# First layer of a two-layer hybrid decoder on one core: the norm's column on ScalarE, low parts issued behind the next block, rope angles mostly on ScalarE, x's sums all on VectorE

## Chip, cores and metric

One Trainium2 chip, one core of it. The metric is the device time of one execution in microseconds (us), as the median of three runs. The profiler records one further execution of the same program.

## What is computed

Two layers over 512 tokens (S) with 2048 features (D). The change lies in the first lines of the first layer; the rest is cut.

```
cos, sin = rope_tables(positions, x.dtype)
c_act = jax.nn.silu(c)
for l in range(DEPTH):
    mod = c_act @ ada_w[l] + ada_b[l]
    shift, scale, gate = [m[:, None, :] for m in jnp.split(mod, 3, axis=-1)]
    h = rms_norm(x, norm_g[l]) * (1.0 + scale) + shift
    z = h @ w_in[l]
    ...      # latent attention and a conv module, both gated, from pieces of z
    y = jnp.concatenate([mla_out, conv_out], axis=-1) @ w_out[l]
    x = x + gate * y
```

## The kernel before

**Layout.** Features lie on the 128 partitions and tokens on the free axis, so x and h are 16 blocks of 128x512, called *columns* here (j from 0 to 15). fp32 products are made of three fp32r matmuls: weights and h are each split into a high part (`hi`, a rounded copy) and a low part (`lo`, the rest), and `mm3` (L249 to L251) adds hi·hi, hi·lo and lo·hi.

**The modulation of a column (layer 0).** `scale0(j)` loads 128 rows of `ada_w` (1 MB) for the scale of column j; `Gemv.block` multiplies them with the broadcast silu(c) and sums, one VectorE instruction (`ada`, L336) and a small one that reads the sum. `make_gs` (L350, `mod<-mod,avec`, 128x1) turns the sum into (1 + scale)·norm_g on VectorE. A second block, `g.block(0, j)`, gives the shift. Then `make_h`: x times gain times 1/rms on VectorE (L356, `x`), the high part with the shift on ScalarE (L357, `h`), the low part on VectorE (L358, `h`), which reads the high part. So each column costs VectorE two blocks, `mod`, `x` and the low part.

**The weights of a column.** `chunk` loads 128x1024 weights (0.5 MB, `raw`), casts them to `hi` on ScalarE in two halves (L242), subtracts for `lo` on GpSimd (L243, the queue that is named SENG) and issues 24 matmuls into 8 PSUM tiles. A *chunk* below is this for one column and one set of 8 output tiles. There are 24: three columns of the first set (K1 = 3), whose sums are then copied out to `held`; eight columns of the gate set (KH = 8), copied out to `part`; then columns 3 to 15 of the first set, added to `held` (L458). `modulate_to` puts the columns ahead of the chunks at rates MR0 and MR, so that a column is made for every one to two chunks.

**The head.** `rope_angles` reduces the position angles on VectorE (13 instructions), `rope_tables` takes two sines on ScalarE. `first_x` squares x's 16 columns on ScalarE and adds them up: the first four on GpSimd, the others on VectorE in two sums. `token_rsqrt_bc` turns the sums into 1/rms (TensorE sums, small VectorE instructions `sm`, `dg`, TensorE again).

**What sets the order.** Each engine runs its own list in order; the lists are made by a scheduler from the order of the code and from its own guess of durations, so a line of code can stand earlier or later on its engine than it was written. All loads go through SyncE's queue in order; `ada` has three buffers, `raw` four, `hi` and `lo` five halves each.

Of the kernel before, what the change touches and what calls it, by code (L numbers as in the profile page):

```python
# [9 lines left out]
F32 = mybir.dt.float32  # L10
# [6 lines left out]
P = 128  # L17
# [33 lines left out]
def hybrid_trunk(ctx, tc, xT, c, pos, invf, vec, adaT, w_s, w_t, w_kr, w_q, w_kv, w_pw, w_o, outT):  # L51
# [22 lines left out]
    def r4(n):  # L74
        return big.tile([P, 2, S], F32R, tag="r4", name=nm(n))
# [43 lines left out]
    def ms(n):  # L119
        return f2(n, "m", NM)  # L120
# [25 lines left out]

    def rope_angles():


        iv = cp.tile([P, 1], F32, tag="iv", name="iv")  # L150
        nc.sync.dma_start(out=iv, in_=invf)
        posi = sp.tile([P, S], I32, tag="t", bufs=3, name="posi")
        nc.sync.dma_start(out=posi, in_=pos.partition_broadcast(P))
        ang, rd = sinT, cosT
        V.tensor_copy(out=ang, in_=posi)
        V.tensor_scalar(out=ang, in0=ang, scalar1=iv, scalar2=None, op0=ALU.mult)
        V.tensor_scalar(out=rd, in0=ang, scalar1=1.0 / TWO_PI, scalar2=MAGIC, op0=ALU.mult, op1=ALU.add)
        V.tensor_scalar(out=rd, in0=rd, scalar1=MAGIC, scalar2=None, op0=ALU.subtract)
        for cc in (C1, C2, C3):
            V.scalar_tensor_tensor(out=ang, in0=rd, scalar=-cc, in1=ang, op0=ALU.mult, op1=ALU.add)  # L160
        V.tensor_scalar(out=ang, in0=ang, scalar1=3.1415925, scalar2=-3.1415925, op0=ALU.min, op1=ALU.max)
        V.tensor_scalar(out=rd, in0=ang, scalar1=-1.0, scalar2=None, op0=ALU.mult)
        V.tensor_max(out=rd, in0=rd, in1=ang)
        V.tensor_scalar(out=rd, in0=rd, scalar1=-1.0, scalar2=math.pi / 2, op0=ALU.mult, op1=ALU.add)
        for p0 in (0, 64):
            V.tensor_scalar(out=ang[p0:p0 + 32], in0=ang[p0:p0 + 32], scalar1=-1.0, scalar2=None, op0=ALU.mult)

    def rope_tables():
        A.activation(out=sinT, in_=sinT, func=AF.Sin)
        A.activation(out=cosT, in_=cosT, func=AF.Sin)  # L170


    def rsqrt_small(x, y, t, scaled=True):
# [190 lines left out]
    def square_sum(acc, x, j, eng=None):  # L364
        if j == 0:
            A.activation(out=acc, in_=x, func=AF.Square)
        else:
            sq = f2("sq")[:, 0:x.shape[1]]
            A.activation(out=sq, in_=x, func=AF.Square)
            (eng or V).tensor_tensor(out=acc, in0=acc, in1=sq, op=ALU.add)  # L370


    def first_x():
        xs = []
        accs = [ms("acc") for _ in range(3)]
        for j in range(0, KC, 2):
            t = r4f("x")
            nc.sync.dma_start(out=t, in_=xT[j:j + 2].rearrange("k p t -> p k t"))
            for e in range(2):

                acc = accs[2] if j < 4 else accs[e]
                square_sum(acc, t[:, e], j + e if j < 4 else j - 4, nc.gpsimd if j < 4 else V)
                xs.append(t[:, e])
        V.tensor_add(out=accs[0], in0=accs[0], in1=accs[2])
        V.tensor_add(out=accs[0], in0=accs[0], in1=accs[1])
        return xs, accs[0]

    def layer(l, xs, rstd, rpsum):
        last = l == DEPTH - 1
# [31 lines left out]
        if l == 0:  # L421
            def modulated(j):
                if j >= EARLY:
                    scale0(j)
                g.block(0, j)
                h.append(make_h(0, j, xs[j], rstd if j else rpsum[0]))

            def park(tiles, where):
                for n in range(8):
                    p = where(n)  # L430
                    (A.copy if n % 2 else V.tensor_copy)(out=p, in_=tiles[n])
                    yield p

            def modulate_to(m):
                while len(h) < min(int(m), KC):
                    if len(h) < NI:
                        with tc.issue_after(rstd_ins.ins):
                            modulated(len(h))
                    else:
                        modulated(len(h))  # L440

            first = [psum(t, "z") for t in tags]
            for j in range(K1):
                modulate_to(j + 1)
                chunk(first, w_first(j), h[j], j == 0, j == K1 - 1)
            held = list(park(first, lambda n: ms("held") if n < 2 else f2("held", "held", 6, sp)))
            mg = [psum(t, "z") for t in tags]
            for j in range(KH):
                modulate_to(max(j + 1, K1 + MR0 * (j + 1)))
                chunk(mg, w_t[l, 0:H, :, j, :].rearrange("a p b -> p a b"), h[j], j == 0, j == KH - 1)  # L450
            part = list(park(mg, lambda n: ms("part")))
            first = [psum(t, "z") for t in tags]
            for j in range(K1, KC):
                modulate_to(max(j + 1, K1 + MR0 * KH + MR * (j + 1 - K1)))
                chunk(first, w_first(j), h[j], j == K1, j == KC - 1)
            krw = kr_weights()
            for n in range(8):
                V.tensor_add(out=held[n], in0=first[n], in1=held[n])  # L458
                first[n] = held[n]
        else:  # L460


            ws = []
            for j in range(2):
                raw = load_w(w_first(j), 8, P)
                ws.append([split_w(raw[:, q:q + 4], SENG, extra[0] if j and q else None) for q in (0, 4)])
                h.append(r4("h"))
            first = [psum(t, "z") for t in tags[:7]]

            def early(n, tk):  # L470
                for j in range(2):
                    hi, lo = ws[j][n // 4]
                    mm3(first[n][:, tk], hi[:, n % 4], lo[:, n % 4], h[j][:, 0, tk], h[j][:, 1, tk], j == 0, False)

            for i, (tk, rs) in enumerate(zip(HALF, rpsum)):
                for j in range(2):
                    make_h(l, j, xs[j], rs if j == 0 else rstd[:, tk], h[j], tk)
                for j in range(2):
                    for n in range(7):
                        hi, lo = ws[j][n // 4]  # L480
# [626 lines left out]
```

## Time and profile before

| | before |
|---|---|
| median of three runs | 1667.66 us (1665.26 to 1672.59) |
| profiled execution, its own time | 1668.02 us |
| span in the profile | 1666.2 us |
| granted TensorE clock, mean of the span | 0.987 |
| busy: TensorE matmul, VectorE, ScalarE, GpSimd | 95%, 74%, 41%, 40% |
| first matmul of a chunk starts, last one of the 24 chunks ends | 34.27 us, 193.43 us |

The span runs from the first to the last instruction; 1.8 us of the time lie around it. A busy TensorE is not one at its peak: its matmuls overlap. Shares over the whole span say little of a change that touches only the first 190 us; that stretch has to be read by itself.

### The profile page before, as it was taken

To read this page: it belongs to the slowest core of one execution; us is meant where nothing else is said; L and a number is where in the kernel's file an instruction comes from. 1 tells how busy PE (TensorE), PEld (TensorE's weight loads), DVE (VectorE), ACT (ScalarE), POOL (GpSimd) and SP (SyncE) were. 2 spreads that over 40 slices of the span, in tenths; PEclk is the share of its full clock that TensorE was granted. 3 is DMA by queue.
4 is the path that set the end of the run, shared out by engine and by line. 5 is a ranking of instruction groups with operands and counts; after the bars stand their busy time and mean duration, and the time that the engine had idled before them with its cause. 6 is when DMAs were issued, how large, how long until landed. Compare 5 with 4: busy or idle time off the path is not lost.

```text
span 1666.2 us, 20654 instructions
## 1 busy us (share of the span) xinstructions
PE 1581.1 (95%) x7350; PEld 1300.9 (78%) x7350; DVE 1226.2 (74%) x2008; ACT 687.4 (41%) x1284; POOL 659.7 (40%) x440
## 2 busy tenths in 40 slices
PE   4988999999999989999999899999999998999999
PEld 2766778877888878788887678888787887888888
DVE  8898897889999558766549675777788787784332
ACT  4222455554654335322223264545445443532221
POOL 2565633425233455666625554331434335100000
PEclk9999999999999999999999999999999999999999
DMA  8877323223233644898936613322332355565441
GB/s 304 287 278 286 135 90 100 70 83 86 76 114 98 231 152 167 287 335 296 322 98 228 246 64 108 92 92 80 99 93 70 104 170 211 177 236 198 151 142 62
DMA packets 82890, 271.53 MB, mean 163 GB/s; under 512 B 10721, under 2 KB 21729, under 8 KB 70241
## 3 DMA queue, kind: packets, MB, share of 16 engines
q1 hardware_dynamic: 82786, 270.20, 48.1%
q8 instruction: 58, 0.95, 0.2%
q14 instruction: 46, 0.38, 0.1%
HBM read 257.55 MB, written 12.62 MB: 162 GB/s over the span
## 4 chain that ended last, share of the span: by engine, by line
PE 62%; DVE 28%; ACT 6%; issue 3%; DMA 1%; POOL 1%; SPq 0%; POOLq 0%; ACTq 0%; DVEq 0%
DVE ada L336 7%; PE wo L250 7%; PE wo L251 7%; PE wo L249 7%; DVE cv L547 5%; PE z L249 4%; PE z L251 4%; PE z L250 4%; PE cg L249 3%; PE cg L251 3%; PE cg L250 3%; PE mg L251 2%; PE mg L249 2%; PE mg L250 2%; DVE x L356 2%
## 5 line engine op out<-in xcount | busy, mean ns | idle before, releaser
L243 POOL TENSOR_TENSOR lo<-raw,hi 128x512 fp32r<-128x512 f32 x380 | 595.2, 1581 | 657.5 <-ACT hi L242 647.3
L242 ACT CAST hi<-raw 128x512 fp32r<-128x512 f32 (+1 forms) x512 | 307.1, 611 | 518.0 <-PE wo L250 209.6
L547 DVE SCALAR_TENSOR_TENSOR cv<-u,lvec,cv 128x512 f32<-128x512 f32 x464 | 348.6, 751 | 7.4
L249 PE MATMUL z<-h,hi 128*128 128x512 f32 (+1 forms) x782 | 305.8, 396 | 17.2 <-ACT h L357 11.0
L251 PE MATMUL z<-h,lo 128*128 128x512 f32 (+1 forms) x782 | 305.8, 391 | 8.3 <-POOL lo L243 8.3
L250 PE MATMUL z<-h,hi 128*128 128x512 f32 (+1 forms) x782 | 304.6, 390 | 0.8 <-DVE h L358 0.7
L336 DVE CUSTOM_DVE_ANT_0 ada<-ada,cb,avec 128x2048 f32<-128x2048 f32 x96 | 257.4, 2682 | 40.5 <-DMA ada<-in_adaT_dram 40.4
L249 PE MATMUL wo<-cat,hi 128*128 128x512 f32 (+1 forms) x544 | 205.8, 378 | 2.0 <-ACT cat L944 2.0
L250 PE MATMUL wo<-cat,hi 128*128 128x512 f32 (+1 forms) x544 | 206.3, 379 | 1.1 <-DVE cat L945 1.0
L251 PE MATMUL wo<-cat,lo 128*128 128x512 f32 (+1 forms) x544 | 205.8, 378 | 0.0
L249 PEld LDWEIGHTS z<-h,hi 128*128 128x128 f32 x782 | 148.5, 191 | 49.2 <-ACT h L357 13.4
L251 PEld LDWEIGHTS z<-h,lo 128*128 128x128 f32 x782 | 148.4, 190 | 42.9 <-POOL lo L243 13.3
L250 PEld LDWEIGHTS z<-h,hi 128*128 128x128 f32 x782 | 148.6, 190 | 29.3 <-DVE h L358 1.8
L243 DVE TENSOR_TENSOR lo<-raw,hi 128x512 fp32r<-128x512 f32 (+1 forms) x132 | 86.3, 655 | 95.0 <-ACT hi L242 94.7
L249 PEld LDWEIGHTS wo<-cat,hi 128*128 128x128 f32 x544 | 102.9, 189 | 21.2 <-ACT cat L944 2.4
L250 PEld LDWEIGHTS wo<-cat,hi 128*128 128x128 f32 x544 | 102.9, 189 | 21.2 <-DVE cat L945 2.3
L251 PEld LDWEIGHTS wo<-cat,lo 128*128 128x128 f32 x544 | 103.0, 189 | 18.8
L249 PE MATMUL cg<-h,hi 128*128 128x512 f32 x256 | 103.0, 402 | 0.0
L250 PE MATMUL cg<-h,hi 128*128 128x512 f32 x256 | 101.5, 397 | 0.0
L251 PE MATMUL cg<-h,lo 128*128 128x512 f32 x256 | 101.5, 396 | 0.0
L780 ACT ACTIVATE pr<-pr,smx,sc 128x128 f32<-128x128 f32 (+1 forms) x64 | 41.9, 654 | 122.8 <-DVE smx L779 122.7
L357 ACT ACTIVATE h<-x,mod 128x512 fp32r<-128x512 f32 (+1 forms) x34 | 23.3, 697 | 136.8 <-DVE mod L336 100.5
(265 smaller groups left out, 2543.4 us busy)
## 6 DMA issues: line engine op xcount, KB each, us to landing
ada<-in_adaT_dram SPq DMA_DIRECT2D x96, 1024.0 KB, 5.7
raw<-in_w_t_dram SPq DMA_DIRECT2D x120, 512.0 KB, 3.8
raw<-in_w_o_dram SPq DMA_DIRECT2D x64, 512.0 KB, 4.6
raw<-in_w_s_dram SPq DMA_DIRECT2D x32, 512.0 KB, 5.9
raw<-in_w_pw_dram SPq DMA_DIRECT2D x16, 512.0 KB, 3.6
raw<-in_w_q_dram SPq DMA_DIRECT2D x24, 256.0 KB, 2.7
x<-in_xT_dram SPq DMA_DIRECT2D x8, 512.0 KB, 6.8
kf<-kfd SPq DMA_DIRECT2D x16, 256.0 KB, 3.7
```

What stands on the lines that cost most here:

```text
L242: A.copy(out=hiv, in_=rawv)
L243: i = eng.tensor_tensor(out=lov, in0=rawv, in1=f(hiv), op=ALU.subtract)
L249: T.matmul(out=ps, lhsT=whi, rhs=mhi, start=start, stop=False)
L250: T.matmul(out=ps, lhsT=whi, rhs=mlo, start=False, stop=False)
L251: T.matmul(out=ps, lhsT=wlo, rhs=mhi, start=False, stop=stop)
L336: V.tensor_tensor_reduce(out=t, in0=t, in1=self.cb, scale=1.0, scalar=vv(l, "ada_b", b), op0=ALU.mult, op1=ALU.add, accum_out=mods[l][:, b ...
L356: V.scalar_tensor_tensor(out=x, in0=x, scalar=gs(l, j), in1=rstd, op0=ALU.mult, op1=ALU.mult)
L357: A.activation(out=hi, in_=x, func=AF.Identity, bias=shift(l, j))
L547: V.scalar_tensor_tensor(out=box[-1], in0=u[:, k:k + S], scalar=w, in1=box[0], op0=ALU.mult, op1=ALU.add)
L780: A.activation(out=pr[:, :n], in_=pr[:, :n], func=AF.Exp, scale=scl, bias=nb, accum_out=sums)
```

## The change

Four edits, all in the head and in layer 0. (1) `scale0` makes the gain on ScalarE (an activation with scale and bias, 128x1) in place of `make_gs` on VectorE. (2) The low part of a column is kept back in `pending` and written in the code after the next column's scale block (`begin`, `settle`). (3) `rope_angles` leaves the first product of the angles to ScalarE and drops the last five VectorE instructions; `rope_tables` does abs, two sines and two negations on ScalarE, issued after the first high part. (4) `first_x` adds all squares on VectorE in two sums; the low parts of the weights of chunk 0 are made on VectorE.

```diff
@@ rope_angles, rope_tables
-        V.tensor_copy(out=ang, in_=posi)
-        V.tensor_scalar(out=ang, in0=ang, scalar1=iv, scalar2=None, op0=ALU.mult)
+        A.activation(out=ang, in_=posi, func=AF.Copy, scale=iv)
...
-        V.tensor_scalar(out=rd, in0=ang, scalar1=-1.0, scalar2=None, op0=ALU.mult)
-        V.tensor_max(out=rd, in0=rd, in1=ang)
-        V.tensor_scalar(out=rd, in0=rd, scalar1=-1.0, scalar2=math.pi / 2, op0=ALU.mult, op1=ALU.add)
+    def rope_tables():
+
+        A.activation(out=cosT, in_=sinT, func=AF.Abs)
+        A.activation(out=cosT, in_=cosT, func=AF.Sin, scale=-1.0, bias=half_pi)
+        A.activation(out=sinT, in_=sinT, func=AF.Sin)
         for p0 in (0, 64):
-            V.tensor_scalar(out=ang[p0:p0 + 32], in0=ang[p0:p0 + 32], scalar1=-1.0, scalar2=None, op0=ALU.mult)
...
+            A.activation(out=sinT[p0:p0 + 32], in_=sinT[p0:p0 + 32], func=AF.Copy, scale=-1.0)
@@ first_x
-                acc = accs[2] if j < 4 else accs[e]
-                square_sum(acc, t[:, e], j + e if j < 4 else j - 4, nc.gpsimd if j < 4 else V)
+                square_sum((acc, acc2)[e], t[:, e], j)
@@ layer
-        def chunk(tiles, src, hj, start, stop):
+        def chunk(tiles, src, hj, start, stop, eng=SENG):
...
+            def begin(j):
+                if j < KC and j == begun[0]:
+                    begun[0] += 1
+                    scale0(j)
...
             def modulated(j):
-                if j >= EARLY:
-                    scale0(j)
+
+                begin(j)
+                settle()
                 g.block(0, j)
-                h.append(make_h(0, j, xs[j], rstd if j else rpsum[0]))
+                t, r = r4("h"), rstd if j else rpsum[0]
+                hi, lo, x = t[:, 0], t[:, 1], xs[j]
+                V.scalar_tensor_tensor(out=x, in0=x, scalar=gs(0, j), in1=r, op0=ALU.mult, op1=ALU.mult)
+                hi_ins[0] = A.activation(out=hi, in_=x, func=AF.Identity, bias=shift(0, j))
+                pending.append(lambda: V.scalar_tensor_tensor(out=lo, in0=x, scalar=shift(0, j), in1=f(hi),
+                                                              op0=ALU.add, op1=ALU.subtract))
+                h.append(t)
...
+                if j == len(h) - 1 and pending:
+                    if j:
+                        begin(j + 1)
+                    settle()
...
-                chunk(first, w_first(j), h[j], j == 0, j == K1 - 1)
+                modulate_to(j + 1, j)
+                if j == 0:
+                    with tc.issue_after(hi_ins[0].ins):
+                        rope_tables()
+                chunk(first, w_first(j), h[j], j == 0, j == K1 - 1, SENG if j else V)
@@ scale0
         g.block(0, 16 + j)
-        make_gs(0, j)
+        n = vv(0, "norm_g", j)
+        A.activation(out=gs(0, j), in_=gs(0, j), func=AF.Identity, scale=n, bias=n)
```

The order that this makes on the engines is shown at three places. In the rows, `ada` is a block (ISA, 128x2048) and the short row behind it reads its sum; line numbers above L154 differ between the two kernels.

**VectorE, columns 0 and 1.** Before, from the scale block of column 1 (`ada_285`):

```order
L336 ISA ada_285,mod_122<-ada_285,cb_126,avec_120 128x2048
L336 ISA mod_122 128x1
L358 SCALAR_TENSOR_TENSOR h_247<-x_144,mod_122,h_247 128x512
L350 SCALAR_TENSOR_TENSOR mod_122<-mod_122,avec_120 128x1
L356 SCALAR_TENSOR_TENSOR x_144<-x_144,mod_122,rstd_208 128x512
L336 ISA ada_289,mod_122<-ada_289,cb_126,avec_120 128x2048
L336 ISA mod_122 128x1
L358 SCALAR_TENSOR_TENSOR h_292<-x_144,mod_122,h_292 128x512
```

and now, from the same block (`ada_284`):

```order
L336 ISA ada_284,mod_118<-ada_284,cb_122,avec_116 128x2048
L336 ISA mod_118 128x1
L439 SCALAR_TENSOR_TENSOR h_241<-x_139,mod_118,h_241 128x512
L336 ISA ada_288,mod_118<-ada_288,cb_122,avec_116 128x2048
L336 ISA mod_118 128x1
L437 SCALAR_TENSOR_TENSOR x_139<-x_139,mod_118,rstd_204 128x512
L336 ISA ada_294,mod_118<-ada_294,cb_122,avec_116 128x2048
L336 ISA mod_118 128x1
L439 SCALAR_TENSOR_TENSOR h_291<-x_139,mod_118,h_291 128x512
```

The `mod` of column 1 is gone, and between column 1's shift block (`ada_288`) and its low part (`h_291`) there now stand `x` and the scale block of column 2 (`ada_294`).

**VectorE, columns 4 and 5.** Before, from the scale block of column 4 (`ada_512`) on:

```order
L336 ISA ada_512,mod_122<-ada_512,cb_126,avec_120 128x2048
L336 ISA mod_122 128x1
L350 SCALAR_TENSOR_TENSOR mod_122<-mod_122,avec_120 128x1
L356 SCALAR_TENSOR_TENSOR x_158<-x_158,mod_122,rstd_208 128x512
L336 ISA ada_516,mod_122<-ada_516,cb_126,avec_120 128x2048
L336 ISA mod_122 128x1
L358 SCALAR_TENSOR_TENSOR h_519<-x_158,mod_122,h_519 128x512
L336 ISA ada_557,mod_122<-ada_557,cb_126,avec_120 128x2048
```

and now, from the same block (`ada_510`) on:

```order
L336 ISA ada_510,mod_118<-ada_510,cb_122,avec_116 128x2048
L336 ISA mod_118 128x1
L437 SCALAR_TENSOR_TENSOR x_151<-x_151,mod_118,rstd_204 128x512
L336 ISA ada_515,mod_118<-ada_515,cb_122,avec_116 128x2048
L336 ISA mod_118 128x1
L439 SCALAR_TENSOR_TENSOR h_518<-x_151,mod_118,h_518 128x512
L336 ISA ada_555,mod_118<-ada_555,cb_122,avec_116 128x2048
```

Only `mod` has gone: the low part of column 4 stands directly behind its own shift block and ahead of the scale block of column 5, as before; columns 5 to 15 read alike, but for column 8, where one copy to `part` stands between the two.

**ScalarE, columns 4 and 5** (`h` is the high part of a column, `hi` the cast of half a chunk's weights). Before, from the high part of column 4:

```order
L357 ACTIVATE h_519<-x_158,mod_122 128x512
L242 CAST hi_570<-raw_568 128x512
L242 CAST hi_586<-raw_568 128x512
L357 ACTIVATE h_564<-x_158,mod_122 128x512
L242 CAST hi_604<-raw_602 128x512
L242 CAST hi_620<-raw_602 128x512
```

and now:

```order
L438 ACTIVATE h_518<-x_151,mod_118 128x512
L1061 ACTIVATE mod_118<-mod_118,avec_116 128x1
L242 CAST hi_568<-raw_566 128x512
L242 CAST hi_584<-raw_566 128x512
L438 ACTIVATE h_563<-x_151,mod_118 128x512
L242 CAST hi_607<-raw_605 128x512
L242 CAST hi_623<-raw_605 128x512
```

The casts keep their places between the high parts, but the first pair now stands behind `mod`, which reads the sum of column 5's scale block.

## Rows read from the trace of the kernel before

**Rows 1.** The page: busy us (share of the span) and instructions of each engine.

```profile
PE 1581.1 (95%) x7350; PEld 1300.9 (78%) x7350; DVE 1226.2 (74%) x2008; ACT 687.4 (41%) x1284; POOL 659.7 (40%) x440
```

**Rows 2.** Windows: us, busy per engine (instructions), granted clock, DMA share, GB/s.

```profile
33.00:110.00 77.00, 66.92 (x269) 52.87 (x270) 68.70 (x61) 22.53 (x39) 43.32 (x22) 0.98 0.84 287
110.00:193.50 83.50, 75.88 (x311) 59.46 (x310) 73.51 (x63) 23.65 (x43) 52.06 (x29) 0.96 0.69 250
```

**Rows 3.** Waits of VectorE, 30 to 195 us: total us, times, longest.

```profile
DVE h L358 <- ACT h L357: 11.9, 15, 0.8
```

**Rows 4.** Groups by line, VectorE, 30 to 187 us: busy us, mean ns.

```profile
L336 DVE CUSTOM_DVE_ANT_0 ada<-ada,cb,avec 128x2048 f32<-128x2048 f32 x31 | 87.1, 2809 | 0.0
L350 DVE SCALAR_TENSOR_TENSOR mod<-mod,avec 128x1 f32<-128x1 f32 x15 | 15.0, 997 | 0.4
```

**Rows 5.** Timeline of column 13, VectorE, with GpSimd's pairs: start us, us.

```profile
159.52 1.12 DVE L350 SCALAR_TENSOR_TENSOR mod<-mod,avec 128x1 f32<-128x1 f32 x1
160.68 0.75 DVE L356 SCALAR_TENSOR_TENSOR x<-x,mod,rstd 128x512 f32<-128x512 f32 x1
161.35 2.35 DVE L336 CUSTOM_DVE_ANT_0 ada<-ada,cb,avec 128x2048 f32<-128x2048 f32 x1
164.49 0.75 DVE L358 SCALAR_TENSOR_TENSOR h<-x,mod,h 128x512 fp32r<-128x512 f32 x1 [0.79 <-ACT h L357]
165.16 3.37 DVE L336 CUSTOM_DVE_ANT_0 ada<-ada,cb,avec 128x2048 f32<-128x2048 f32 x1
...
155.99 4.64 POOL L243 TENSOR_TENSOR lo<-raw,hi 128x512 fp32r<-128x512 f32 x2 [3.50 <-ACT hi L242]
165.04 7.57 POOL L243 TENSOR_TENSOR lo<-raw,hi 128x512 fp32r<-128x512 f32 x4 [4.42 <-ACT hi L242]
```

**Rows 6.** Timeline around column 3, VectorE, and one GpSimd instruction.

```profile
58.20 0.15 DVE L350 SCALAR_TENSOR_TENSOR mod<-mod,avec 128x1 f32<-128x1 f32 x1
60.53 1.77 DVE L356 SCALAR_TENSOR_TENSOR x<-x,mod,rstd 128x512 f32<-128x512 f32 x1
63.10 0.91 DVE L358 SCALAR_TENSOR_TENSOR h<-x,mod,h 128x512 fp32r<-128x512 f32 x1 [0.79 <-ACT h L357]
...
61.72 1.75 POOL L243 TENSOR_TENSOR lo<-raw,hi 128x512 fp32r<-128x512 f32 x1
```

**Rows 7.** Timeline of the head, and the page's group of low parts on VectorE.

```profile
22.44 0.69 DVE L385 TENSOR_TENSOR acc<-acc,acc 128x512 f32<-128x512 f32 x1
23.19 1.87 PE L194 MATMUL st<-ones,acc 128*128 128x1 f32 x8 [9.22 <-DVE acc L385]
25.44 1.09 DVE L350 SCALAR_TENSOR_TENSOR mod<-mod,avec 128x1 f32<-128x1 f32 x1
26.53 1.23 DVE L176 TENSOR_SCALAR sm<-sm 128x4 int32<-128x4 int32 x1
32.71 0.75 DVE L356 SCALAR_TENSOR_TENSOR x<-x,mod,stb 128x512 f32<-128x512 f32 x1 [0.57 <-ACT rstd L222]
...
L243 DVE TENSOR_TENSOR lo<-raw,hi 128x512 fp32r<-128x512 f32 (+1 forms) x132 | 86.3, 655 | 95.0 <-ACT hi L242 94.7
```

**Rows 8.** Timeline: scale sums of columns 4 and 15, last matmuls of the chunks.

```profile
67.25 0.07 DVE L336 DVE_READ_ACCUMULATOR2_ANT mod<- 128x1 f32 x1
179.54 0.07 DVE L336 DVE_READ_ACCUMULATOR2_ANT mod<- 128x1 f32 x1
192.81 0.39 PE L250 MATMUL z<-h,hi 128*128 128x512 f32 x1
193.04 0.39 PE L251 MATMUL z<-h,lo 128*128 128x512 f32 x1
```

**Rows 9.** Groups of ScalarE: one element per partition, and 128.

```profile
L780 ACT ACTIVATION_READ_ACCUMULATOR pr<-pr,smx,sc 128x1 f32 x64 | 12.0, 187 | 0.0
L782 ACT ACTIVATE pr<-pr,smx 128x128 f32<-128x128 f32 x16 | 6.4, 400 | 2.0 <-DVE smx L781 2.0
```

**Rows 10.** DMA issues, 33 to 190 us: KB each, median us to landing.

```profile
raw<-in_w_s_dram SPq DMA_DIRECT2D x14, 512.0 KB, 6.2
```

More of the change, by code (lines that the diff above doesn't have):

```diff
@@ L161, in rope_angles @@
         V.tensor_scalar(out=ang, in0=ang, scalar1=3.1415925, scalar2=-3.1415925, op0=ALU.min, op1=ALU.max)
-        V.tensor_scalar(out=rd, in0=ang, scalar1=-1.0, scalar2=None, op0=ALU.mult)
-        V.tensor_max(out=rd, in0=rd, in1=ang)
-        V.tensor_scalar(out=rd, in0=rd, scalar1=-1.0, scalar2=math.pi / 2, op0=ALU.mult, op1=ALU.add)
+    half_pi = cp.tile([P, 1], F32, tag="half_pi", name="half_pi")
+    V.memset(half_pi, math.pi / 2)
+    def rope_tables():
+        A.activation(out=cosT, in_=sinT, func=AF.Abs)
+        A.activation(out=cosT, in_=cosT, func=AF.Sin, scale=-1.0, bias=half_pi)
+        A.activation(out=sinT, in_=sinT, func=AF.Sin)
         for p0 in (0, 64):
-            V.tensor_scalar(out=ang[p0:p0 + 32], in0=ang[p0:p0 + 32], scalar1=-1.0, scalar2=None, op0=ALU.mult)
-    def rope_tables():
-        A.activation(out=sinT, in_=sinT, func=AF.Sin)
-        A.activation(out=cosT, in_=cosT, func=AF.Sin)
+            A.activation(out=sinT[p0:p0 + 32], in_=sinT[p0:p0 + 32], func=AF.Copy, scale=-1.0)
     def rsqrt_small(x, y, t, scaled=True):
@@ L374, in first_x @@
         xs = []
-        accs = [ms("acc") for _ in range(3)]
+        acc, acc2 = ms("acc"), ms("acc2")
         for j in range(0, KC, 2):
@@ L379, in first_x @@
             for e in range(2):
-                acc = accs[2] if j < 4 else accs[e]
-                square_sum(acc, t[:, e], j + e if j < 4 else j - 4, nc.gpsimd if j < 4 else V)
+                square_sum((acc, acc2)[e], t[:, e], j)
                 xs.append(t[:, e])
-        V.tensor_add(out=accs[0], in0=accs[0], in1=accs[2])
-        V.tensor_add(out=accs[0], in0=accs[0], in1=accs[1])
-        return xs, accs[0]
+        V.tensor_add(out=acc, in0=acc, in1=acc2)
+        return xs, acc
     def layer(l, xs, rstd, rpsum):
@@ L395, in layer @@
         tags = [t for t in ("mm", "up", "s", "cv", "pz") for _ in range(NB[t])]
-        def chunk(tiles, src, hj, start, stop):
+        def chunk(tiles, src, hj, start, stop, eng=SENG):
             raw = load_w(src, 8, P)
             for q in (0, 4):
-                hi, lo = split_w(raw[:, q:q + 4], SENG)
+                hi, lo = split_w(raw[:, q:q + 4], eng)
                 for n in range(4):
@@ L421, in layer, with settle @@
         if l == 0:
+            pending, begun = [], [EARLY]
+            def begin(j):
+                if j < KC and j == begun[0]:
+                    begun[0] += 1
+                    scale0(j)
+            def settle():
+                while pending:
+                    pending.pop()()
             def modulated(j):
-                if j >= EARLY:
-                    scale0(j)
+                begin(j)
+                settle()
                 g.block(0, j)
-                h.append(make_h(0, j, xs[j], rstd if j else rpsum[0]))
+                t, r = r4("h"), rstd if j else rpsum[0]
[5 more added lines that the diff above has]
+                h.append(t)
+            hi_ins = [None]
             def park(tiles, where):
@@ L432, in park, with modulate_to @@
                     yield p
-            def modulate_to(m):
+            def modulate_to(m, j):
                 while len(h) < min(int(m), KC):
@@ L440, in modulate_to @@
                         modulated(len(h))
+                if j == len(h) - 1 and pending:
+                    if j:
+                        begin(j + 1)
+                    settle()
             first = [psum(t, "z") for t in tags]
             for j in range(K1):
-                modulate_to(j + 1)
-                chunk(first, w_first(j), h[j], j == 0, j == K1 - 1)
+                modulate_to(j + 1, j)
[3 more added lines that the diff above has]
+                chunk(first, w_first(j), h[j], j == 0, j == K1 - 1, SENG if j else V)
             held = list(park(first, lambda n: ms("held") if n < 2 else f2("held", "held", 6, sp)))
@@ L448, in layer @@
             for j in range(KH):
-                modulate_to(max(j + 1, K1 + MR0 * (j + 1)))
+                modulate_to(max(j + 1, K1 + MR0 * (j + 1)), j)
                 chunk(mg, w_t[l, 0:H, :, j, :].rearrange("a p b -> p a b"), h[j], j == 0, j == KH - 1)
@@ L453, in layer @@
             for j in range(K1, KC):
-                modulate_to(max(j + 1, K1 + MR0 * KH + MR * (j + 1 - K1)))
+                modulate_to(max(j + 1, K1 + MR0 * KH + MR * (j + 1 - K1)), j)
                 chunk(first, w_first(j), h[j], j == K1, j == KC - 1)
@@ L1041, in hybrid_trunk @@
     state = (xs, rstd0, [token_rsqrt_bc(acc, D, rstd0)])
-    rope_tables()
     rstd_ins = bc_ins[0]
```

## Prediction

> **What bounds the kernel now.** The page comes first: TensorE is 95% busy over the span, VectorE 74% [rows 1]. For this change the average is of no use, since all that is edited lies ahead of 193.43 us [rows 8]. So I cut that stretch into windows. From 33 to 110 us VectorE is busy 68.70 of 77.00 us, from 110 to 193.5 us 73.51 of 83.50 [rows 2]: some 89%. TensorE shows 66.92 and 75.88, but its matmuls overlap. The starts of its last two lie 0.23 us apart [rows 8], so the 24 chunks of 24 matmuls need 576 x 0.23 = 132 us of the 159 us from the first of them at 34.27 us to the last at 193.43 us. VectorE sets the pace; TensorE has some 27 us of idle time and of slower matmuls.
>
> What does VectorE lose? Two things. The list of its waits shows 11.9 us in 15 waits of 0.79 us: the low part waits until ScalarE has made the high part of the same column [rows 3]. And by the groups, a block takes 2.81 us in the mean, the 128x1 `mod` 1.00 us [rows 4]. The timeline tells why: a block takes 2.35 or 3.37 us [rows 5], `mod` 0.15 us while GpSimd is idle and 1.12 us behind a GpSimd pair [rows 5, 6]. Each is longer by about 1.0 us when a GpSimd subtraction is pending. In column 13 the pair that began at 155.99 ends with the slow `mod`; the next `x` takes its plain 0.75 [rows 5]. With GpSimd idle, `mod` took 0.15, and the `x` two instructions on paid, with 1.77 us [rows 6]. So the price belongs to the GpSimd instruction, not to the VectorE instruction that it meets. One case costs little: the subtraction from 61.72 to 63.47 us ran mostly under the 0.79 us wait, and the low part took 0.91 us, 0.16 more than 0.75 [rows 5, 6].
>
> The Trainium skill has this as a rule (SBUF, "Who interferes with whom"): a VectorE instruction with two SBUF inputs and a GpSimd instruction that reads SBUF take the shared pair of ports one after the other, for a whole instruction each. It speaks against this change, since a 128x1 `mod` that leaves VectorE does not take the GpSimd instruction with it. The trace agrees on who pays, with 0.97 to 1.02 us per stall. In the sum below the rule would alter nothing, as both sides hold the same number of stalls.
>
> **The change part by part.**
>
> *Head.* VectorE has its last sum at 23.13 us now [rows 7]. With two sines off the middle of ScalarE's squares and one closing addition of 0.69 us less, and with four more additions on VectorE, which has that time once seven angle instructions (some 5.5 us) are gone, I put it about 1.0 us earlier. The chain behind it then loses the `mod` of 1.09 us, and some 1.0 us of the 1.23 us of `sm`, one more stall beside GpSimd [rows 7], since the low parts of chunk 0 no longer run there; so -2.1 us. But the first block, which overlapped TensorE's 1.87 us of sums, now stands behind them, +1.9, and the two low parts on VectorE, 0.655 us each [rows 7], stand ahead of `x`, +1.3, of which the 0.57 us wait there covers a part. Sum: -1.0 - 2.1 + 1.9 + 1.3 - 0.6 = -0.5, and I take **-0.4**. The sines now run behind the first high part on ScalarE, some 3 us, under two blocks of VectorE; without that cover `mod` 1 would be late by up to 1 us.
>
> *Columns 0 to 3* (`x` of column 0 to the scale sum of column 4: 32.71 to 67.32 us, 34.6 us [rows 7, 8]). The printed order shows the low part of column 1 behind the next block, and that of column 3 behind a copy: two waits of 0.79 us go [rows 3]. Four `mod` go, at 0.15 + 0.08 us of gaps [rows 5, 6] = 0.9; their stalls stay, since GpSimd's pairs stay. TensorE ends chunk 2 earlier, and the waits of the copies for it (1.2 us) go by half. Sum **-3.1**.
>
> *Columns 4 to 14.* Here the order says that the edit does not reach: the low part stands directly behind its own shift block and still waits for ScalarE. What changes is that `mod` is gone, that `x` now waits for ScalarE's `mod`, and that the casts stand behind that. The wait of `x` is not in the trace. The bounds for the activation are 0.187 us for one element per partition and 0.400 us for 128 [rows 9]; nearer to the first, I take 0.28, and 0.07 for two handoffs, as in 0.79 for an activation of 0.72: 0.35 us, from 0.26 to 0.47. Now one column with one chunk. Before, column 13: 1.16 (`mod`, stalled) + 0.79 (`x`) + 2.27 + 0.79 (wait) + 0.75 + 3.29 (block, stalled) = 9.05 us [rows 5]. After: `x` waits 0.35 and takes 0.75; the casts come right behind `mod`, so the first subtraction stalls the shift block, 1.02 + 2.27; the second is pending when that ends and runs under the wait for the high part, so that this costs 1.05 (1.02 and a handoff) in place of 0.79; low part 0.75, scale block 2.27. Sum 8.46, 0.59 less. With a second chunk in the column two more subtractions cost about 1.0 us each on both sides. Some columns of before are short already (their pair fell elsewhere), so I take 0.55 x 11 = **-6.0**. Bounds of one column: +0.12 if neither subtraction falls under a wait (0.35 for 0.23), and about -1.2 if both do.
>
> The Trainium skill gives ScalarE a fixed cost per instruction (VectorE: DVE Perf Modes, "The TRN2 errata"): 224 cycles and one for each element, at 1.2 GHz. By it the 128x1 activation would be 0.19 us, an estimate, and each exposed wait 0.26: up to 1 us less in the sum. No row here shows that instruction.
>
> *End* (scale sum of column 15 to the last matmul, 179.61 to 193.43, 13.8 us [rows 8]). Chunk 14's casts move behind the `mod` of column 15, so its matmuls start about 1.0 us after that sum rather than ahead of it; 48 x 0.23 = 11 us and 1 to 2 us of waits for low parts follow: 13.7 to 15. I take **+0.5**.
>
> Sum: -0.4 - 3.1 - 6.0 + 0.5 = -9.0 us. Behind 193 us no engine's order differs, so the gain should be carried to the end. The profiled execution took 1668.02 us, 0.36 above the median: 1668.0 - 9.0 = **1659.0 us**. About 0.5% (8.3 us) is what a measurement of this kernel can tell from no change; the border lies at 1659.3.
>
> **Rivals.**
> - *The columns give nothing back.* The new wait of `x` is exposed in each column and the second subtraction misses the wait: 11 x 0.12 = +1.3, so -0.4 - 3.1 + 1.3 + 0.5 = -1.7, 1666.3 us. For it: the rows show one subtraction under a wait, and that between two others [rows 6]. Against it: the casts now come 3 us ahead of the high part.
> - *The 15.0 us of `mod` [rows 4] go whole,* because GpSimd gets most of its work done in the waits: -15.0, +5.3 for 15 waits of 0.35, -1.6 for the two low parts, -8.4 for 0.76 in each of 11 columns: 19.7 us less (head and end cancel), 1648.3. Against it: the stall moved on to `x` [rows 6].
> - *Slower: a cast holds up the high part.* On ScalarE the casts of a chunk now stand between `mod` and the high part of the same column. Their weights are issued when the scale block of the column before has freed its buffer, some 8 us ahead of the next scale sum, and land after 6.2 us in the median [rows 10]. The high part is needed 4.4 us behind that sum and two casts take 1.1 us, so a column is held up from a landing time of 8 + 4.4 - 1.1 = 11.3 us on, and the gain is gone if each of the 11 loses 0.8 us, from 12.1 us on. At 13 us each loses 1.7: -9.0 + 18.7, 1677.7 us. Against it: six microseconds is half of that.
> - *Taken back later:* layer 0's attention or the load queue absorbs the shift. Nothing behind 193 us is tied to a fixed time; half of the gain lost would be 1663.5.
>
> **How the numbers follow.** The sum as worked out 55%, with its own range 1654.5 to 1662 (0.33 below the border, 0.22 above); columns give nothing 18%; `mod` whole 15%; taken back later 6%; slower 6%. Faster by over 0.5%: 0.33 + 0.15 = 0.48. Within: 0.22 + 0.18 + 0.06 = 0.46. Slower: 0.06. The range leaves out the slower case and half of the case of 1648.3: 1650 to 1666.5.
>
> **What would show it.** `mod` gone from VectorE, and ScalarE's 128x1 activation near 0.28 us. The waits of low parts for ScalarE still there some 11 to 12 times, and a new list entry of `x` waiting for `mod`. Blocks with a stall still at 3.3 to 3.4 us, but more low parts at about 0.9 to 1.0 us. The scale sum of column 15 near 170.5 us, the last matmul of the chunks near 184.5. I am wrong if the stalls get fewer by much more than one per column, if ScalarE's casts show waits for DMA ahead of a high part, or if the first 193 us shrink and the time doesn't.

## The result and the profile after

The median went from 1668.65 to 1655.57 us (four runs of each). The ratio is 0.9918, 95% interval 0.9889 to 0.9947: 0.8% faster. Ratios leave out two slow executions, one of the changed kernel (1750.13 us, granted clock 0.851; the other three have a median of 1655.04) and one of e8 below (3155.82 us). 1659.0 was predicted, with 1650 to 1666.5 as the range. The profiled execution took 1655.04 us, its span 1653.2: 13.0 less than before, where the sum said 9.0.

The page's busy line answers to [rows 1], the two windows to [rows 2] (about the same pieces of work, which now end at 104 and 180.2 us).

```profile
PE 1574.6 (95%) x7350; PEld 1295.9 (78%) x7350; DVE 1208.3 (73%) x1991; ACT 694.7 (42%) x1304; POOL 664.4 (40%) x435
```

```profile
33.00:104.00 71.00, 65.69 (x267) 51.32 (x268) 65.03 (x54) 27.85 (x53) 48.06 (x23) 1.00 0.94 329
104.00:180.20 76.20, 72.80 (x312) 57.60 (x311) 64.48 (x54) 25.24 (x49) 60.10 (x29) 1.00 0.72 261
```

In the second window VectorE is busy 85%, where it had 88%. The waits of VectorE from 28 to 190 us (total us, times, longest) answer to [rows 3]:

```profile
DVE h L439 <- ACT h L438: 9.9, 14, 0.8
DVE x L437 <- ACT mod L1061: 5.0, 11, 0.5
```

Two more groups of the kernel before, from the same list as [rows 4] (busy us, mean ns | idle before):

```profile
L356 DVE SCALAR_TENSOR_TENSOR x<-x,mod,rstd 128x512 f32<-128x512 f32 x15 | 21.2, 1415 | 0.5
L358 DVE SCALAR_TENSOR_TENSOR h<-x,mod,h 128x512 fp32r<-128x512 f32 x16 | 13.4, 835 | 11.9 <-ACT h L357 11.9
```

and the groups of VectorE and ScalarE now, 30 to 187 us:

```profile
L336 DVE CUSTOM_DVE_ANT_0 ada<-ada,cb,avec 128x2048 f32<-128x2048 f32 x31 | 94.4, 3046 | 0.0
L437 DVE SCALAR_TENSOR_TENSOR x<-x,mod,rstd 128x512 f32<-128x512 f32 x15 | 16.0, 1068 | 5.0 <-ACT mod L1061 5.0
L439 DVE SCALAR_TENSOR_TENSOR h<-x,mod,h 128x512 fp32r<-128x512 f32 x16 | 14.7, 917 | 9.9 <-ACT h L438 9.9
...
L1061 ACT ACTIVATE mod<-mod,avec 128x1 f32<-128x1 f32 x15 | 5.8, 387 | 44.3 <-DVE mod L336 44.3
```

The new wait of `x` is there, 0.46 us each. ScalarE's `mod` takes 0.387 us, close to the upper bound of [rows 9] and not to the lower one that was taken. The blocks became *dearer*, 3.05 us in the mean for 2.81: with the 12.7 us of stalls that `mod` took gone, 7.3 us more fall on them. Column 13, the timeline that answers to [rows 5]:

```profile
148.00 0.07 DVE L336 DVE_READ_ACCUMULATOR2_ANT mod<- 128x1 f32 x1
148.53 0.75 DVE L437 SCALAR_TENSOR_TENSOR x<-x,mod,rstd 128x512 f32<-128x512 f32 x1 [0.46 <-ACT mod L1061]
149.19 3.37 DVE L336 CUSTOM_DVE_ANT_0 ada<-ada,cb,avec 128x2048 f32<-128x2048 f32 x1
152.50 0.08 DVE L336 DVE_READ_ACCUMULATOR2_ANT mod<- 128x1 f32 x1
153.37 0.90 DVE L439 SCALAR_TENSOR_TENSOR h<-x,mod,h 128x512 fp32r<-128x512 f32 x1 [0.79 <-ACT h L438]
154.19 3.38 DVE L336 CUSTOM_DVE_ANT_0 ada<-ada,cb,avec 128x2048 f32<-128x2048 f32 x1
157.50 0.08 DVE L336 DVE_READ_ACCUMULATOR2_ANT mod<- 128x1 f32 x1
158.03 1.24 DVE L437 SCALAR_TENSOR_TENSOR x<-x,mod,rstd 128x512 f32<-128x512 f32 x1 [0.46 <-ACT mod L1061]
...
149.08 4.64 POOL L243 TENSOR_TENSOR lo<-raw,hi 128x512 fp32r<-128x512 f32 x2 [3.83 <-ACT hi L242]
153.92 9.80 POOL L243 TENSOR_TENSOR lo<-raw,hi 128x512 fp32r<-128x512 f32 x4 [0.20 <-ACT hi L242]
```

Four subtractions meet VectorE here. Two lengthen a block by 1.0 us each. The other two run mostly under a wait: the low part takes 0.90 us, 0.15 too much, and the last `x` 1.24, 0.49 too much. The marks that answer to [rows 7, 8], with the last chunk matmul:

```profile
30.92 1.29 DVE L243 TENSOR_TENSOR lo<-raw,hi 128x512 fp32r<-128x512 f32 x2
32.12 0.74 DVE L437 SCALAR_TENSOR_TENSOR x<-x,mod,stb 128x512 f32<-128x512 f32 x1
62.69 0.08 DVE L336 DVE_READ_ACCUMULATOR2_ANT mod<- 128x1 f32 x1
166.46 0.08 DVE L336 DVE_READ_ACCUMULATOR2_ANT mod<- 128x1 f32 x1
...
179.86 0.39 PE L251 MATMUL z<-h,lo 128*128 128x512 f32 x1
```

So by stretch, predicted and measured:

| stretch | before | after | measured | predicted |
|---|---|---|---|---|
| start to `x` of column 0 | 32.71 | 32.12 | -0.6 | -0.4 |
| to the scale sum of column 4 | 34.5 | 30.6 | -4.0 | -3.1 |
| to the scale sum of column 15 | 112.3 | 103.8 | -8.5 | -6.0 |
| to the end of the last chunk matmul | 13.9 | 13.8 | -0.1 | +0.5 |
| rest of the span | 1472.8 | 1472.9 | 0.1 | 0 |

All four terms erred to the same side, by 4 us in sum; none made up for another.

Below, *stall* is what blocks, `x`, low parts and `mod` take in that list of groups beyond 2.345, 0.75, 0.75 and 0.15 us apiece. Before it is (87.1 - 72.7) + (21.2 - 11.25) + (13.4 - 12.0) + (15.0 - 2.25) = 38.5 us, now 21.7 + 4.75 + 2.7 = 29.1. (For e4 it is reckoned from count times mean, since blocks that follow each other directly overlap in the busy sum.) The waits for ScalarE went from 12.5 (with 0.6 for `rstd`) to 14.9.

### The profile page after: what moved, and what is told of

Its sections match the earlier page's. It is cut to its first block, busy times and chain, and to the rows that moved or that the text cites. A ratio compares the mean times of both kernels' runs of the same rounds, so it can differ in the third digit from the quotient of the medians.

```text
span 1653.2 us, 20647 instructions
## 1 busy us (share of the span) xinstructions
PE 1574.6 (95%) x7350; PEld 1295.9 (78%) x7350; DVE 1208.3 (73%) x1991; ACT 694.7 (42%) x1304; POOL 664.4 (40%) x435
## 4 chain that ended last, share of the span: by engine, by line
PE 61%; DVE 29%; ACT 6%; issue 3%; DMA 1%; POOL 1%; SPq 0%; POOLq 0%; ACTq 0%; DVEq 0%
DVE ada L336 8%; PE wo L250 7%; PE wo L251 7%; PE wo L249 7%; DVE cv L571 5%; PE z L251 4%; PE z L250 4%; PE z L249 4%; PE cg L249 3%; PE cg L251 3%; PE cg L250 3%; PE mg L251 2%; PE mg L249 2%; PE mg L250 2%; DVE pr L800 1%
## 5 line engine op out<-in xcount | busy, mean ns | idle before, releaser
L243 POOL TENSOR_TENSOR lo<-raw,hi 128x512 fp32r<-128x512 f32 x378 | 603.9, 1612 | 648.2 <-ACT hi L242 639.0
L336 DVE CUSTOM_DVE_ANT_0 ada<-ada,cb,avec 128x2048 f32<-128x2048 f32 x96 | 266.5, 2776 | 41.1 <-DMA ada<-in_adaT_dram 41.1
L804 ACT ACTIVATE pr<-pr,smx,sc 128x128 f32<-128x128 f32 (+1 forms) x64 | 41.9, 654 | 122.6 <-DVE smx L803 122.4
L251 PE MATMUL mg<-h,lo 128*128 128x512 f32 x192 | 76.1, 396 | 2.3 <-POOL lo L243 2.3
```

The source lines that it names most:

```text
L251: T.matmul(out=ps, lhsT=wlo, rhs=mhi, start=False, stop=stop)
L336: V.tensor_tensor_reduce(out=t, in0=t, in1=self.cb, scale=1.0, scalar=vv(l, "ada_b", b), op0=ALU.mult, op1=ALU.add, accum_out=mods[l][:, b ...
L804: A.activation(out=pr[:, :n], in_=pr[:, :n], func=AF.Exp, scale=scl, bias=nb, accum_out=sums)
```

## Experiments

Each compares with runs of the kernel before on the same chip. Stall and wait are those of VectorE, from the list of groups and of waits of the profiled execution; "last" is where the last chunk matmul ends.

| kernel | median us | ratio (95% interval) | last | stall | wait |
|---|---|---|---|---|---|
| before | 1668 to 1670 | 1 | 193.4 | 38.5 | 12.5 |
| after | 1655.57 | 0.9918 (0.9889 to 0.9947) | 180.2 | 29.1 | 14.9 |
| e2 only the gain moved | 1657.57 | 0.9931 (0.9914 to 0.9948) | 182.2 | 25.1 | 18.0 |
| e1 all but the gain | 1663.99 | 0.9964 (0.9953 to 0.9976) | 189.7 | 39.7 | 9.9 |
| e3 before without the gain | 1661.94 | 0.9960 (0.9945 to 0.9975) | 187.9 | 33.4 | 12.5 |
| e4 low parts behind the next block | 1653.52 | 0.9904 (0.9885 to 0.9922) | 176.2 | 39.1 | 0.8 |
| e6 low parts at once | 1659.05 | 0.9934 (0.9917 to 0.9951) | 181.9 | 25.2 | 17.4 |
| e7 casts behind the high part | 1659.74 | 0.9940 (0.9926 to 0.9953) | 185.4 | 29.7 | 14.9 |
| e5 old head | 1654.52 | 0.9916 (0.9900 to 0.9932) | 180.9 | 28.7 | 15.5 |
| e9 after, subtractions on VectorE | 1646.27 | 0.9863 (0.9845 to 0.9880) | 169.4 | 0 | 5.6 |
| e10 e4, subtractions on VectorE | 1645.15 | 0.9861 (0.9841 to 0.9880) | 167.8 | 0 | 0 |
| e11 before, subtractions on VectorE | 1642.17 | 0.9841 (0.9824 to 0.9858) | 166.6 | 0 | 0 |

**The theory** was that of the prediction: each GpSimd subtraction costs VectorE about 1 us wherever it meets it, unless it runs under a wait; the casts, now ahead of the high part, put subtractions under the waits. The rivals were that `mod` itself was the price, and that the reordered low parts or the head gave the gain.

**e2: the kernel before with edit (1) alone.**

```diff
     def scale0(j):
         g.block(0, 16 + j)
-        make_gs(0, j)
+        n = vv(0, "norm_g", j)
+        A.activation(out=gs(0, j), in_=gs(0, j), func=AF.Identity, scale=n, bias=n)
```

> The kernel before with one edit alone: the gain of a column on ScalarE. Theory: columns 4 to 14 run as in the changed kernel, about 8.5 us less, head and first columns nearly as before: 1657 to 1661. Rival (the new wait of 0.46 us a column outweighs 0.23 us of VectorE work): 1667 to 1672.

As the theory had it: 102.8 us from the scale sum of column 4 to that of column 15, where the changed kernel takes 103.8. One line gives 11.2 of the 13.2 us at the end of the chunks. Its waits (28 to 190 us) are longer than before by 5.5 us, its stalls less by 13.4:

```profile
DVE h L358 <- ACT h L357: 11.9, 15, 0.8
DVE x L356 <- ACT mod L1037: 5.5, 12, 0.5
```

**e1: the changed kernel with the gain back on VectorE.**

```diff
-        n = vv(0, "norm_g", j)
-        A.activation(out=gs(0, j), in_=gs(0, j), func=AF.Identity, scale=n, bias=n)
+        make_gs(0, j)
```

> The changed kernel with one edit undone: the gain of a column is made on VectorE again. Theory (the gain of the change comes from where the casts, and with them GpSimd's subtractions, fall: behind ScalarE's mod one subtraction runs under the wait for the high part and one under the wait for the gain): without the ScalarE mod the casts follow the high part again, stalls of blocks and of mod come back, columns 4 to 14 take about 112 us as before instead of 104, time 1663 to 1667. Rival (only the VectorE work of mod counts, 0.23 us a column less 0.46 of new wait): undoing it costs nothing or gains 2 us, 1653 to 1657.

As the theory had it: columns 4 to 14 take 111.5 us. Edits (2) to (4) alone leave 0.36%, and the stalls are about those of before. `mod` pays again, in the list of groups:

```profile
L350 DVE SCALAR_TENSOR_TENSOR mod<-mod,avec 128x1 f32<-128x1 f32 x15 | 15.9, 1062 | 0.5
```

**e3: the kernel before without the gain instruction at all.**

```diff
     def scale0(j):
         g.block(0, 16 + j)
-        make_gs(0, j)
```

> The kernel before without the instruction that makes the gain in layer 0: it leaves out (1 + scale) times norm_g there and multiplies x by the scale's sum. No wait for ScalarE takes its place. Theory (a stall belongs to GpSimd's subtraction and passes to the next VectorE instruction): only 0.15 us of work and its gaps go in each of 15 columns, x takes the stalls: 3 to 5 us less, 1663 to 1665.5. Rival (mod's measured 1.00 us in the mean is its own price): 15 us less, 1653.

Between the two, nearer to the theory: the median of 1661.94 us is 7.6 below the kernel before in these runs, where 3 to 5 were expected and 15 by the rival, and the last chunk matmul is 5.5 us earlier. `mod`'s 12.7 us of stalls are gone, and 7.6 are back elsewhere: `x` has 3.9 more than before, blocks 3.0, low parts 0.7. So most of the price is GpSimd's, not `mod`'s, though not all of it comes back. That the kernel which makes no gain at all is not faster than e2, which makes it on ScalarE, says what the moved instruction brings: the wait behind it. The waits of `x` add 5.5 us in e2, and its stalls are 8.3 us less than in e3.

```profile
L336 DVE CUSTOM_DVE_ANT_0 ada<-ada,cb,avec 128x2048 f32<-128x2048 f32 x31 | 90.1, 2908 | 0.0
L358 DVE SCALAR_TENSOR_TENSOR h<-x,mod,h 128x512 fp32r<-128x512 f32 x16 | 14.1, 881 | 11.9 <-ACT h L357 11.9
L356 DVE SCALAR_TENSOR_TENSOR x<-x,mod,rstd 128x512 f32<-128x512 f32 x15 | 25.1, 1674 | 0.4
```

**e4: every low part of a column forced behind the next scale block** (`g.last` is the newest block).

```diff
...
             def settle():
                 while pending:
-                    pending.pop()()
+                    with tc.issue_after(g.last.ins):
+                        pending.pop()()
```

> The changed kernel with the low part of every column held behind the next column's scale block by an issue order, as the code is written; VectorE then waits neither for high parts nor for gains. Theory (a wait is where a subtraction of GpSimd runs almost free; without waits each of the 46 costs a full 1.0 us): some 14 us of waits go and 46 x 1.0 - 29 = 17 us of stalls come, 1655 to 1660. Rival (the 15 us of waits in the changed kernel are lost time): 1641 to 1645.

The waits are gone, 14.1 us of them, and 10.0 us came back as stalls: without waits little is left for a subtraction to run under. The theory had put 17 us, 1.0 for each of the 46; the stalls come to 0.85 apiece, and the median lies 1.5 us below its range, well above the rival's. Late in the columns a low part and the `x` behind it each pay a whole one (timeline):

```profile
152.30 1.76 DVE L440 SCALAR_TENSOR_TENSOR h<-x,mod,h 128x512 fp32r<-128x512 f32 x1
153.99 1.77 DVE L438 SCALAR_TENSOR_TENSOR x<-x,mod,rstd 128x512 f32<-128x512 f32 x1
```

The chunks end 4.0 us earlier than in the changed kernel; the rest of the profiled span was longer by as much (1477.4 for 1472.9). The intervals of the two ratios overlap.

**e6: the low part written at once, as before, in the changed kernel.**

```diff
-                pending.append(lambda: V.scalar_tensor_tensor(out=lo, in0=x, scalar=shift(0, j), in1=f(hi),
-                                                              op0=ALU.add, op1=ALU.subtract))
+                V.scalar_tensor_tensor(out=lo, in0=x, scalar=shift(0, j), in1=f(hi), op0=ALU.add, op1=ALU.subtract)
```

> The changed kernel with the low part of a column written in the code right behind its high part, as before; gain on ScalarE and the head stay. Theory (the order of the engine was altered by this edit in columns 1, 3 and 8 alone): two or three waits of 0.79 us come back, 1656 to 1658.5. Rival (the edit is what brought the gain): back by 6 us and more, 1661 and above.

Edit (2) is worth 1.6 us at the end of the chunks, through columns 1 and 3. The median is 0.5 us above the theory's range; against the changed kernel the two intervals overlap, so by the time it is not resolved.

**e7: the casts held behind the newest high part.**

```diff
             for q in (0, 4):
-                hi, lo = split_w(raw[:, q:q + 4], eng)
+                if l == 0 and len(h) > 1:
+                    with tc.issue_after(hi_ins[0].ins):
+                        hi, lo = split_w(raw[:, q:q + 4], eng)
...
```

> The changed kernel with the casts of each chunk behind the first held until the newest high part is issued, so that on ScalarE they follow the high part, as before, and no longer stand between the gain and the high part; VectorE's order is that of the changed kernel. Theory A, that of the prediction (the casts behind the gain bring a subtraction under the wait for the high part): that is lost, columns 4 to 14 take 6 to 8 us more, 1661 to 1664. Theory B (a subtraction that is pending runs under whichever wait comes next, for the high part or for the gain): per two columns some 0.3 us more, 1655 to 1658.

The median lies between the two ranges. Columns 4 to 14 take 105.1 us, 1.3 more than in the changed kernel: about the 1.6 of theory B, not the 6 to 8 of theory A. The stalls hardly change. With the casts behind the high part, a subtraction now runs under each of the eleven waits of `x` (`x` at 1.22 or 1.23 us; in the changed kernel under six), and under fewer of those of low parts:

```profile
L441 DVE SCALAR_TENSOR_TENSOR x<-x,mod,rstd 128x512 f32<-128x512 f32 x15 | 18.4, 1224 | 5.0 <-ACT mod L1065 5.0
```

Of the 5.2 us that the chunks end later, 3.5 lie behind the scale sum of column 15, where the casts of the last chunks come late. That end was in neither theory. So it is not the place of the casts but the wait as such that takes up a subtraction; this part of the prediction was too narrow.

**e5: the changed kernel with the old head** (angles, sines, four squares on GpSimd, and chunk 0's low parts on GpSimd; the last line of the edit, the others put back what the diff of the change took out of the head):

```diff
-                chunk(first, w_first(j), h[j], j == 0, j == K1 - 1, SENG if j else V)
+                chunk(first, w_first(j), h[j], j == 0, j == K1 - 1)
```

> The changed kernel with the head of the kernel before: angles and sines as they were, four squares added on GpSimd, the low parts of chunk 0 on GpSimd. Theory: the new head is worth little (x of column 0 started 0.6 us earlier in the changed kernel, and 0.4 was predicted), and of the first three columns it holds the low parts of chunk 0, four half chunks in number with the two of the angles' place, at about 1 us each: x of column 0 near 32.7 us, the last matmul of the chunks at 181 to 183 us, 1656 to 1659 us (before is about 1669 here). Rival: the new head is the larger part of the gain, since the columns only follow what the head gave: 1662 us or more, with the last matmul at 187 us or later.

`x` of column 0 starts at 32.76 us, as the theory had it, and the chunks end 0.6 us later than in the changed kernel, at 180.9; 181 to 183 had been put, and the median is 1.5 us below the range. The ratio is that of the changed kernel: edits (3) and (4) can't be told from nothing.

**e9: the changed kernel with all subtractions of layer 0's chunks on VectorE.**

```diff
-        def chunk(tiles, src, hj, start, stop, eng=SENG):
+        def chunk(tiles, src, hj, start, stop, eng=SENG if l else V):
...
```

> The changed kernel with all low parts of layer 0's chunks on VectorE and else as it is. Theory: the 28 us of stalls go and 28 us of work come, the waits stay: no change within 3 us, 1652 to 1658. Rival (work on the bounding engine costs its own time, stalls are hidden): 1670 and above.

Wrong: it takes some 9 us off the changed kernel. The exchange of stalls for work came out as put. The 29.1 us of stalls go, and the 46 further subtractions take about 0.62 us of VectorE each from one start to the next (in the timeline of e11 below a pair starts at 138.96 and the next instruction at 140.17), 28.5 us. What failed is "the waits stay". VectorE now has subtractions to do while ScalarE works, and its waits (28 to 190 us) fall from 14.9 to 5.6:

```profile
DVE x L437 <- ACT mod L1061: 3.2, 7, 0.5
DVE h L439 <- ACT h L438: 2.4, 3, 0.8
```

The same edit on e4 (**e8**) gave 1646.12 us, ratio 0.9858 (0.9840 to 0.9876), in its expected range; no trace of it is read here, and the kernel ran again as **e10**.

> The kernel with the low part of every column behind the next block (no waits for ScalarE), and all low parts of layer 0's chunks on VectorE, so that GpSimd has no subtraction there. Theory (a subtraction costs VectorE 0.83 us in stalls in that order, and 0.66 us if VectorE does it): 38 us of stalls go, 46 x 0.62 = 28 us of work come, VectorE 10 us less; TensorE's 132 us of matmuls from 33.8 us on then bound the stretch, so 5 to 8 us less than with GpSimd, 1645 to 1649. Rival (28 us more work on the engine that bounds): 1665 and above.

> Low parts of columns forced behind the next scale block, and every low part of layer 0's chunks on VectorE: the kernel that gave a ratio of 0.9858, run again for a trace. Theory (each of the two edits takes away the same waits of VectorE, so the second adds little to the other): 1644 to 1649 us, VectorE waits for ScalarE under 2 us in all, all blocks at 2.35 us, the last matmul of the chunks within 3 us of the 169.4 us that the changed kernel with the subtractions alone showed. Rival: the two add up, since the 3.2 and 2.4 us of waits that were left there go too: the last matmul at 164 us or earlier and 1642 us or less.

The theory for e10 holds: no stalls, no waits for ScalarE, and the last chunk matmul only 1.6 us earlier than in e9.

**e11: the kernel before with this edit alone.**

```diff
-                hi, lo = split_w(raw[:, q:q + 4], SENG)
+                hi, lo = split_w(raw[:, q:q + 4], V if l == 0 else SENG)
```

> The kernel before with one edit alone: every low part of layer 0's chunks on VectorE in place of GpSimd; the gain stays on VectorE and each low part of a column keeps its place. Theory (what the change gained was time that VectorE lost to GpSimd's subtractions): without them the change has little left to give. mod then costs 0.15 us and 0.08 of gaps in each column in place of 1.0, and 0.46 us of waits for ScalarE are absent, so this kernel should come out within 4 us of the changed kernel with the same edit (ratio 0.9863 there): 1644 to 1652 us, blocks at 2.35 us and x at 0.75 throughout. Rival: the change is worth its 13 us by itself (fewer instructions and waits on VectorE, whatever GpSimd does), so the kernel before with this edit stays about 13 us above the changed one with it: 1658 us or more.

The fastest of all by the median, 1.6% below the kernel before, with nothing of the studied change in it; its interval overlaps those of e9 and e10. The rival is out, and the median is 1.8 us below the theory's range: `x` of column 0 starts 2.0 us earlier than before, at 30.66, since two stalls in the head are gone too (`mod` 0.16 us for 1.09, `sm` 0.16 for 1.23, [rows 7]). Groups of VectorE, 30 to 187 us, then one column with two chunks (timeline), then TensorE's groups from 32.2 to 166.7 us:

```profile
L336 DVE CUSTOM_DVE_ANT_0 ada<-ada,cb,avec 128x2048 f32<-128x2048 f32 x31 | 72.7, 2346 | 0.0
L243 DVE TENSOR_TENSOR lo<-raw,hi 128x512 fp32r<-128x512 f32 (+1 forms) x51 | 33.3, 691 | 0.0
L358 DVE SCALAR_TENSOR_TENSOR h<-x,mod,h 128x512 fp32r<-128x512 f32 x16 | 11.9, 746 | 0.0
L356 DVE SCALAR_TENSOR_TENSOR x<-x,mod,rstd 128x512 f32<-128x512 f32 x15 | 11.3, 751 | 0.4
```

```profile
135.83 0.16 DVE L350 SCALAR_TENSOR_TENSOR mod<-mod,avec 128x1 f32<-128x1 f32 x1
136.02 0.75 DVE L356 SCALAR_TENSOR_TENSOR x<-x,mod,rstd 128x512 f32<-128x512 f32 x1
136.69 2.34 DVE L336 CUSTOM_DVE_ANT_0 ada<-ada,cb,avec 128x2048 f32<-128x2048 f32 x1
138.96 0.08 DVE L336 DVE_READ_ACCUMULATOR2_ANT mod<- 128x1 f32 x1
138.96 1.29 DVE L243 TENSOR_TENSOR lo<-raw,hi 128x512 fp32r<-128x512 f32 x2
140.17 0.75 DVE L358 SCALAR_TENSOR_TENSOR h<-x,mod,h 128x512 fp32r<-128x512 f32 x1
140.83 1.29 DVE L243 TENSOR_TENSOR lo<-raw,hi 128x512 fp32r<-128x512 f32 x2
142.03 2.35 DVE L336 CUSTOM_DVE_ANT_0 ada<-ada,cb,avec 128x2048 f32<-128x2048 f32 x1
144.31 0.08 DVE L336 DVE_READ_ACCUMULATOR2_ANT mod<- 128x1 f32 x1
```

```profile
L250 PE MATMUL z<-h,hi 128*128 128x512 f32 x192 | 75.4, 393 | 0.0
L251 PE MATMUL z<-h,lo 128*128 128x512 f32 x192 | 74.8, 392 | 0.0
L249 PE MATMUL z<-h,hi 128*128 128x512 f32 x192 | 73.7, 401 | 2.4 <-ACT h L357 2.4
```

`mod` is back at 0.16 us, every block at 2.35, the wait for the high part is covered by two subtractions, and TensorE runs its 576 matmuls in 134 us, with 2.4 us of waits in this list. In e10 they take 134 us as well, near the 132 that the prediction worked out for TensorE alone, so VectorE no longer sets the pace there. What the change worked around is gone, and so is its use.

## Why the prediction was right, and where its sizes were off

**What bounds, and who pays.** Right. VectorE set the pace, and a stall belongs to the pending GpSimd instruction: with `mod` back on VectorE (e1) it pays 1.06 us, with `mod` gone and no wait in its place (e3) `x` pays 1.67, and with the waits gone (e4) a low part pays 1.76. The Trainium skill's rule (SBUF, "Who interferes with whom") stood against a whole gain of `mod`, and the trace agrees: of `mod`'s 12.7 us of stalls, 7.6 came back in e3.

**Head, -0.4.** Right, -0.6; e5 shows that it cannot be told from nothing in the time.

**Columns 0 to 3, -3.1.** Right in kind; -4.0. The wait of the copies for TensorE went whole (1.2 us), not by half. Of the two waits of low parts one went whole, the other is 0.19 us long.

**Columns 4 to 14, -6.0.** The mechanism was right in part, the term too small: -8.5. In these eleven columns, summed from the same instructions of both traces, stalls went from 31.1 to 22.2 us (-8.9), the waits of `x` from 0.35 to 4.56 (+4.2), those of low parts from 8.7 to 8.1 (-0.6), those of the copies to `part` from 1.2 to 0 (-1.2), and `mod`'s own 0.15 us apiece and its gaps are gone (-2.0): -8.5. The prediction's column, 0.59 us less, holds a loss of 0.71 of stalls, where 0.81 was measured; it counted no gain at the copies, and took off half a microsecond that it need not have. The step that failed in size: "the first subtraction stalls the shift block ... the second ... runs under the wait for the high part". The second did, and cheaper than put (0.79 + 0.15 for 1.05). But in six of the eleven columns another ran under the *new* wait too: `x` at 1.23 or 1.24 us, 0.49 of stall in place of 1.0. The wait that the change adds was priced as a pure loss: six times 0.51 us came back, 3.1 of the 4.6 us. And the reason that the prediction gave, the casts' new place, was not needed for most of it: with the casts behind the high part again (e7) these columns still take 7.2 us less than before.

**ScalarE's `mod`, 0.28, and the wait, 0.35.** Too low: 0.387 and 0.46, at the upper bounds (0.400 and 0.47). The Trainium skill's rule (VectorE: DVE Perf Modes, "The TRN2 errata") would have 0.19, an estimate; for this activation, whose scale and bias are both read from 128x1 operands, the measurement decides against it.

**End, +0.5; nothing taken back.** -0.1, and the rest of the span is the same to 0.1 us. Of the marks foretold, the scale sum of column 15 "near 170.5" should by the prediction's own terms have been 170.1 (it came at 166.46), and the waits of low parts were 14, two of them of 0.19 us, for 11 to 12.

**The rivals.** "Columns give nothing back" (1666.3) is out by the interval. "`mod` goes whole" (1648.3) needs its stalls to vanish; in e3 they did not. "A cast holds up the high part": ScalarE's list of waits has no cast that waits for a load any more. "Taken back later" did not happen.

**Still open.** In the profiled executions the rest of the span behind the chunks lies between 1469.6 us (e5) and 1478.9 (e3, whose own time was 6.8 above its median), with the same work in it. That is why a gain of 4 us at the chunks, as in e4, need not show in one execution. The clock records of the traces point to a cause. In the rest of the span TensorE had the lower of its two granted levels (1.2 GHz in place of 2.4) for 23.9 us in e5 and 41.9 in e3; by an estimate, half of these 18.0 us is lost work, 9.0, and the two differ by 9.3. For the changed kernel and e4 it is 30.7 and 37.5 us, 3.4 of the 4.5 by which they differ. Not every kernel follows (e9: 27.3 us at the lower level and a rest of 1475.1), and no run tested it.

## To carry to other kernels

When an instruction takes 1.0 us more in some places than in others, find the instruction on the other engine that is pending there, and price *that* one on both engines: here the 48 subtractions cost VectorE 38.5 us of stalls when GpSimd made them, and about 30 us when VectorE made them itself (e11); and these 30 us also filled the 12.5 us that VectorE had waited for ScalarE. An engine's waits and its stalls belong in one sum, because a stall that falls under a wait is cheaper (0.15 us for one of 0.79, 0.49 for one of 0.46, in place of 1.0); an edit that adds a wait can so gain, and one that takes waits away can lose most of its worth (e4). Try the one-line edit alone before a change of four parts: e2 holds most of this one, and e11 more than all of it.

## What had not been expected of the hardware

A 128x1 activation with scale and bias from memory took 0.387 us, about as long as a 128x128 one (0.400, [rows 9]), while the same arithmetic on VectorE took 0.16 us with GpSimd quiet. Without GpSimd's subtractions in the stretch, VectorE's instructions all ran at one length: 31 blocks at 2.346 us in the mean, where the kernel before had 2.81. And the granted clock of the two windows rose from 0.98 and 0.96 to 1.00, and TensorE's waits ahead of its matmuls fell from 18.7 to 10.8 us. No run separates what the clock gave; VectorE, which set the pace, waited 5.6 us for TensorE before and 2.8 after (28 to 190 us), so by these waits at most 2.8 of the 13 us can have come from TensorE.
